# New durations in a list scheduler, a charge for changes of TensorE's tile configuration, and a mask matmul padded from 42 to 128 rows

## The chip, the core and the metric

The kernel runs on one core of one Trainium2 chip. The metric is device time in microseconds (us), the median of three executions of the whole kernel.

## What is computed

The reference is a two-layer backbone over 1024 latent tokens and 256 context tokens of width 1024, all in float32. Cut to one layer:

```python
u = modulate(rms_norm(h, norm1_g), mod[0], mod[1])          # latent and context, own modulation
pa, pb, pc, pd = split(u @ w_in)                            # four head groups
ya = ssd_bidir(conv_silu(pa))        # Mamba-2 SSD, chunks of 128, forward and backward
yb = block_attention(rope(rms_norm(q)), rope(rms_norm(k)), v)          # grouped-query, 4 heads
yc = gelu(gate) * (rglru(forward) + rglru(backward))        # RG-LRU, a linear scan
yd = diff_attention(q, k, v)         # softmax(q1 k1) v - lam * softmax(q2 k2) v, 4 heads
h = h + mod[2] * (concat(ya, yb, yc, yd) @ w_out)
h = h + mod[5] * (square(relu(modulate(rms_norm(h, norm2_g), mod[3], mod[4]) @ w_mlp1)) @ w_mlp2)
```

Inside the SSD each chunk needs `exp(a_cum[l] - a_cum[s])` under a triangular mask, and `exp(a_cum)` alone.

## The kernel before

Every float32 matrix is split into a high and a low part in a rounded format (`F32R`), and a product is the sum of three matmuls: high by high, high by low, low by high. `gemm_fm` and `gemm_tm` issue these in groups of three, 512 or 256 columns wide; the two layers hold 18,456 recorded matmuls. The other matmuls (transposes, SSD, P times V, sums of squares) stay in plain float32.

The program first records all operations in program order as a graph (`Sched.op`). Then `Sched.run` plays the graph through a model of five engines (PE is TensorE, DVE VectorE, ACT ScalarE, POOL GpSimd, SP the queue of DMA issues). At each model time every free engine takes, from the operations whose predecessors are done and whose buffers can be given, the one with the smallest latest start (`pri`, worked out backwards in `due` from TensorE's own order). The order in which operations are taken is the order in which the instructions are issued; on the chip each engine then works through its own list in that order, and semaphores enforce the dependencies. So the model's durations never become time directly. They only set the order on each engine, which engine takes an operation that either ACT or DVE can do (`either`), and which buffer a tile gets.

The model's prices stand in `act_cost`, `dve_cost`, `mm_cost` and `mms`; the latency from one engine to the next is the `gap` in `run` (0 on one engine, 200 ns where TensorE is on either side, else `LAT`), and `HOP` is the latency that `due` assumes. An operation that both ACT and DVE can do is skipped by one engine where the other would be done sooner, with ACT's duration weighted by 1.0 and DVE's by 1.6 (`PREF`).

A layer runs in this order, with neighbours overlapped as far as the graph and the buffers allow: norm, RG-LRU projections, RG-LRU, query, key and value projections, SSD for two groups, then attention in two rounds of one grouped-query and one differential head pair each (`G1D1`, `G0D0`), the output projection, norm, MLP. In time, layer 0's projections, LRU and SSD lie at about 20 to 450 us, its attention at 450 to 800, output projection and MLP (and the start of layer 1) up to about 1850; for layer 1 the same stretches are 1850 to 2250, 2250 to 2550, and 2550 to the end.

The mask matmul is in `ssd_group`, once per chunk of 128 tokens and group: `pick` (a column of an identity, in two copies, spread over 128 columns) times `acr`, which holds the cumulated decays, their high parts in rows 0 to 9 and their low parts in rows 32 to 41. It brings one chunk's row of decays to all 128 partitions. Its two operands are 42 rows high.

"Tile configuration" is the part of the 128 by 128 array that a matmul uses: its height is 32, 64 or 128 rows and its width 32, 64 or 128 columns, the next that holds the operand. Most matmuls are 128 by 128; P times V, parts of the SSD and of the attention's output use 64 columns, the sums of squares and the modulation 32 columns, the mask matmul 64 rows.

Of the kernel before, what the change touches and what calls it, by code (L numbers as in the profile page):

```python
# [11 lines left out]
F32R = mybir.dt.float32r  # L12
# [141 lines left out]


class Sched:
    LAT = 150.0
    HOP = 220.0
    STRETCH = 1.5
    TABLES = {AF.Sqrt: 1, AF.Exp: 0, AF.Tanh: 0, AF.Abs: 0}  # L160
    PREF = dict(ACT=1.0, DVE=1.6)
# [124 lines left out]
        self.ops.append(o)  # L286
        return o

# [1 line left out]
    def act_cost(self, out, in_, func, **kw):  # L290
        n = max(out.n(), in_.n())
        aps = sum(isinstance(kw.get(k), _V) for k in ("scale", "bias"))
        return (52 if in_.t.cls == "psum" else 94) + n / 1.2 + 93 * aps + (93 if "accum_out" in kw else 0)

    def act(self, out, in_, func, **kw):
        return self.op("ACT", [("activation", dict(out=out, in_=in_, func=func, **kw))],
# [2 lines left out]
    def dve_cost(self, method, fast=False, n=None, **kw):  # L299
        if n is None:  # L300
            n = max(x.n() for x in kw.values() if isinstance(x, _V))
        rate = 0.521 if fast else 1.0417
        if method == "reciprocal":
            rate = 6.25
        aps = sum(isinstance(kw.get(k), _V) for k in ("scalar", "scalar1", "scalar2"))
        return 69 + rate * n + 61 * aps

    def dve(self, method, fast=False, n=None, **kw):
        return self.op("DVE", [(method, kw)], self.dve_cost(method, fast, n, **kw))
# [56 lines left out]
    def mm_cost(self, rhs):  # L366
        n = rhs.n()
        if rhs.dt == F32R:
            return 2.5 + (n / 2.4 if n >= 256 else n * 4 / 2.4)
        return 2.5 + max(n * 4 / 2.4, 187)  # L370

    def mms(self, calls, par=1):
        cost = sum(self.mm_cost(c["rhs"]) for c in calls) / par
        return self.op("PE", [("matmul", c) for c in calls], cost + 10)

    def transposes(self, calls):
        return self.op("PE", [("transpose", c) for c in calls], 109.0 * len(calls))

# [1 line left out]
    def due(self):  # L380
        ops = self.ops
        end = [0.0] * len(ops)
# [31 lines left out]
    def run(self, trace=None):  # L414
        self.due()
        ops = self.ops
        n = len(ops)
# [26 lines left out]
        releases = []  # L444
        t = 0.0
        table = 0
        done = 0
        last_t = 0.0

# [37 lines left out]
        while done < n:  # L487
            progress = False
            while releases and releases[0][0] <= t:
                _, cn, slot, s = heapq.heappop(releases)  # L490
                c = self.classes[cn]
                c["live"][s] -= 1
                if cn == "psum":
                    c["busy"] = [None if x is slot else x for x in c["busy"]]
                else:
                    c["free"].append((t, slot))
            for e in names:
                if free[e] > t:
                    continue
                f = fut[e]  # L500
                while f and f[0][0] <= t:
                    _, pri, i = heapq.heappop(f)
                    if ops[i].t0 is None:
                        heapq.heappush(avail[e], (pri, i))
                skipped = []
                pick = None
                while avail[e]:
                    pri, i = heapq.heappop(avail[e])
                    if ops[i].t0 is not None:
                        continue  # L510
                    o = ops[i]
                    if any(max(t, free[a], o.ready[a]) + o.alts[a][1] * self.PREF[a] < t + o.alts[e][1] * self.PREF[e]
                           for a in o.alts if a != e):
                        skipped.append((pri, i))
                        continue
                    if not o.new or can_alloc(o):
                        pick = i
                        break
                    skipped.append((pri, i))
                for x in skipped:  # L520
                    heapq.heappush(avail[e], x)
                if pick is None:
                    continue
                o = ops[pick]
                o.eng = e
                o.calls, o.cost = o.alts[e]
                progress = True
                if e == "ACT":
                    need = self.TABLES.get(o.calls[0][1].get("func"))
                    if need is not None and need != table:  # L530
                        table = need
                        o.cost += 1283.0
                for tl in o.new:
                    self._alloc(tl)
                    if tl.cls != "dram":
                        c = self.classes[tl.cls]
                        c["live"][tl.stream] += 1
                        heads[tl.cls, tl.stream] += 1
                self._emit(o)
                o.t0 = t  # L540
                free[e] = t + o.cost
                if o.nbytes:
                    begin = max(dma_free, t + 1100)
                    dma_free = begin + o.nbytes / 360.0
                    end = dma_free + 850.0
                else:
                    end = t + o.cost
                if trace is not None:
                    trace.append((t, end, o))
                done += 1  # L550
                for j in start_succ[pick]:
                    p = ops[j]
                    p.left -= 1
                    for a in p.alts:
                        p.ready[a] = max(p.ready[a], t)
                        if p.left == 0:
                            heapq.heappush(fut[a], (p.ready[a], p.pri, j))
                for j in o.succs:
                    p = ops[j]
                    p.left -= 1  # L560
                    for a in p.alts:
                        gap = 0 if a == e and not o.nbytes else 200 if "PE" in (a, e) else self.LAT
                        p.ready[a] = max(p.ready[a], end + gap)
                        if p.left == 0:
                            heapq.heappush(fut[a], (p.ready[a], p.pri, j))
                for tl in o.tiles:
                    tl.ops_left -= 1
                    tl.end = max(tl.end, end)
                    if tl.ops_left == 0 and tl.slot is not None:
                        heapq.heappush(releases, (tl.end + self.LAT, tl.cls, tl if tl.cls == "psum" else tl.slot, tl.stream))  # L570
                last_t = max(last_t, end)
            if progress:
                continue
            nxt = [free[e] for e in names if free[e] > t and (avail[e] or fut[e])]
            nxt += [fut[e][0][0] for e in names if fut[e] and fut[e][0][0] > t]
            if releases:
                nxt.append(max(releases[0][0], t))
            nxt = [x for x in nxt if x > t]
            if not nxt:
                raise RuntimeError("no operation can be issued")  # L580
            t = min(nxt)
# [66 lines left out]
class Trunk:  # L648
# [23 lines left out]
        self.s.cls(cn, self.sb, 1, n)  # L672
        return self.s.tile(cn, n, dt, "", name, rows)

# [1 line left out]
    def setup(self):  # L676
        s, A = self.s, self.A
        self.cst = self.const(448, "cst")
        s.dma(self.cst.v, A["cst"])
        c = self.cst  # L680
        self.ident, self.mf, self.mb = c[:, 0:128], c[:, 128:256], c[:, 256:384]
        self.blk2, self.inv_ln, self.inv128 = c[:, 384:386], c[:, 386:387], c[:, 387:388]
        self.nhalf, self.tiny, self.ones32 = c[:, 388:404], c[:, 404:405], c[:, 406:438]
        self.pick = self.const(10, "pick", dt=F32R)[0:42, :]
        s.copy("DVE", self.pick, c[0:42, 438:448])
        self.cT = self.const(8 * 32, "cT")
        self.consts_a(0)
        x = s.tile("h", 512, F32, "load", "cx")
# [185 lines left out]
        b = 48 * si + 8 * m + k  # L874
        return self.L[l]["mod"][:, b:b + 1]

# [1 line left out]
    def split_w(self, raw, n):  # L878
        s = self.s
        hi = s.tile("w", WW, F32R, "", "wh")  # L880
# [55 lines left out]
                   dict(out=o, lhsT=ul, rhs=wh[:, b:b + m], start=False, stop=(k == 7))])  # L936
        return bank

# [1 line left out]
    def load_x(self, gi):  # L940
        s, A = self.s, self.A
        if gi == 0:
# [102 lines left out]
                s.dma(x[:, NL:NT], y[:, CO:CW].f)  # L1045
        self.mixd[k] = d

# [1 line left out]
    def conv(self, out, raw, wcols, bcol, W=CW):  # L1049
        s = self.s  # L1050
        o = out[:, 0:W]
# [24 lines left out]
             300)  # L1076
        return raw

# [1 line left out]
    def lru_weights(self, l):  # L1080
        s, A = self.s, self.A
        bd = s.tile("S", SW, F32, "lru", "bd")
# [69 lines left out]
        s.stt(wv, wv, 0.5, g, ALU.mult, ALU.mult)  # L1152
        self.split_mix(4 + ct, w, wy, "lru")

# [1 line left out]
    def ssd_dt(self, l, dtraw):  # L1156
        s, L = self.s, self.L[l]
        c = self.ssdc
# [16 lines left out]
        s.act(w1, w1, AF.Exp)  # L1175
        s.tt(te, w1, dt, ALU.mult)
        R = s.tile("S", SW, F32R, "ssdr", "acr")
        s.op("POOL", [("memset", dict(ap=R[0:42, 0:1024].f, constant=0.0))], 1300)
        n4 = nac.r("p (t d g h) -> p g d h t", t=10, d=2, g=2)
        for g in range(2):  # L1180
            pb = s.tile("psum", 512, F32, "ssd", "par")
# [8 lines left out]
    def ssd_group(self, l, g, xs, B, C, zmake):  # L1190
# [37 lines left out]
        for i, c in enumerate(order):  # L1228
# [3 lines left out]
            E, ex, cf = wk[:, 0:512], wk[:, 512:768], wk[:, 768:1024]  # L1232
            CE = E
            pb = s.tile("psum", 512, F32, "ssd", "pbc")
            s.mms([dict(out=pb.v, lhsT=self.pick[:, c:c + 1].bc([42, 128]), rhs=self.acr[0:42, 512 * g:512 * g + 512],
                        start=True, stop=True)])
            s.act(E, pb.v, AF.Exp)
            for hh in range(2):
# [54 lines left out]
            s.stt(yy, yy, L["sng"][:, g:g + 1], pb[:, 0:128 * n], ALU.mult, ALU.mult)  # L1293
        self.split_mix(g, y, W, "ssd")

# [1 line left out]
    def qk_post(self, l, bank, off, H, d, gain, t, dst, rq=None):  # L1297
        s = self.s
        n = H * d
# [71 lines left out]
        if name == "dtq":  # L1371
            self.ssd_dt(l, dtraw)

# [1 line left out]
    def att_open(self, l, kind, idx):  # L1375
        s, qd = self.s, self.qd
        gqa = kind == "gqa"
# [149 lines left out]
                yield (blk + i / len(sts)) / nblk  # L1527
                self.att_block(st, blk, nblk)

# [1 line left out]
    def out_proj(self, l, gis, ks):  # L1531
        s = self.s
        n = NT if l == 0 else NL
# [240 lines left out]
```

## Time and profile before

| | before |
|---|---|
| median of 3 executions | 3346.67 us (3345.6, 3346.67, 3353.66) |
| span of the profiled execution | 3352.2 us |
| time of the profiled execution | not listed apart; 3353.66 is the only one of the three that is longer than the span |
| TensorE busy | 3258.6 us (97%), 18,456 matmuls |
| VectorE busy | 2171.1 us (65%) |
| ScalarE busy | 1166.4 us (35%) |
| GpSimd busy | 147.1 us (4%) |
| mean granted clock of TensorE | 0.990 |

The profile is of one execution. A matmul's end is modelled: it is listed longer than the time until the next one starts, so neighbouring matmuls overlap in it, and a stretch in which TensorE counts as busy may still hold lost time. The distance from one start to the next shows what a matmul costs in a stream.

### The profile page before, as it was taken

To read this page: it belongs to the slowest core of one execution; us is meant where nothing else is said; L and a number is where in the kernel's file an instruction comes from. 1 tells how busy PE (TensorE), PEld (TensorE's weight loads), DVE (VectorE), ACT (ScalarE), POOL (GpSimd) and SP (SyncE) were. 2 spreads that over 40 slices of the span, in tenths; PEclk is the share of its full clock that TensorE was granted. 3 is DMA by queue.
4 is the path that set the end of the run, shared out by engine and by line. 5 is a ranking of instruction groups with operands and counts; after the bars stand their busy time and mean duration, and the time that the engine had idled before them with its cause. 6 is when DMAs were issued, how large, how long until landed. Compare 5 with 4: busy or idle time off the path is not lost. (4 is left out here: it accounts for less than half of the span.)

```text
span 3352.2 us, 45841 instructions
## 1 busy us (share of the span) xinstructions
PE 3258.6 (97%) x18456; PEld 2622.8 (78%) x18456; DVE 2171.1 (65%) x3785; ACT 1166.4 (35%) x2026; POOL 147.1 (4%) x168
## 2 busy tenths in 40 slices
PE   8999989999999999999999999999999999999999
PEld 6877786677688888887887888886677788888887
DVE  4787789894565555554556688689883655555554
ACT  5554447772311110101112554438771311111111
POOL 0010040000000000000000010030000000000000
PEclk9999999999999999999999989989999999999999
DMA  8443261416212222212110321151433111111111
GB/s 247 140 125 97 89 175 41 110 35 232 70 48 75 72 79 67 78 57 85 42 45 26 118 73 50 57 154 39 97 116 121 41 51 51 51 44 46 49 50 57
DMA packets 253868, 276.51 MB, mean 82 GB/s; under 512 B 22876, under 2 KB 212184, under 8 KB 253656
## 3 DMA queue, kind: packets, MB, share of 16 engines
q1 hardware_dynamic: 253656, 273.59, 27.0%
q8 instruction: 145, 2.38, 0.3%
q14 instruction: 67, 0.55, 0.1%
HBM read 218.75 MB, written 54.79 MB: 82 GB/s over the span
## 5 line engine op out<-in xcount | busy, mean ns | idle before, releaser
L606 DVE SCALAR_TENSOR_TENSOR hR<-banks,mod,hR 128x512 f32<-128x512 f32 x720 | 497.2, 697 | 420.4 <-PE banks L606 420.4
L606 PE MATMUL banks<-uh,wh 128*128 128x512 f32 (+1 forms) x1808 | 682.4, 377 | 5.8 <-ACT cvr L606 1.9
L606 PE MATMUL banks<-uh,wl 128*128 128x512 f32 (+1 forms) x1808 | 669.1, 370 | 1.7 <-DVE wl L606 1.7
L606 PE MATMUL banks<-ul,wh 128*128 128x512 f32 (+1 forms) x1808 | 669.0, 370 | 1.3 <-DVE ul L606 1.2
L606 ACT ACTIVATE wh<-wr 128x1024 fp32r<-128x1024 f32 (+2 forms) x193 | 189.5, 992 | 1050.7 <-PE banks L606 1009.9
L606 PE MATMUL banks<-hh,wh 128*128 128x512 f32 (+1 forms) x1280 | 476.7, 372 | 0.0
L606 PE MATMUL banks<-hl,wh 128*128 128x512 f32 (+1 forms) x1280 | 475.5, 371 | 0.0
L606 PE MATMUL banks<-hh,wl 128*128 128x512 f32 (+1 forms) x1280 | 474.8, 371 | 0.0
L606 PEld LDWEIGHTS banks<-uh,wh 128*128 128x128 f32 x1808 | 341.3, 189 | 98.8 <-issue 26.1
L606 PEld LDWEIGHTS banks<-uh,wl 128*128 128x128 f32 x1808 | 340.6, 188 | 65.4 <-DVE wl L606 3.0
L606 PEld LDWEIGHTS banks<-ul,wh 128*128 128x128 f32 x1808 | 341.1, 189 | 61.5 <-DVE ul L606 3.7
L606 DVE TENSOR_SCALAR_CACHE_REDUCE P<-banks,rq 128x1280 f32<-128x1280 f32 (+1 forms) x216 | 301.3, 1427 | 29.4 <-PE banks L606 28.1
L606 DVE TENSOR_TENSOR r<-r 128x512 f32<-128x512 f32 x160 | 102.2, 639 | 333.6 <-ACT r L606 331.4
L606 PEld LDWEIGHTS banks<-hh,wh 128*128 128x128 f32 x1280 | 240.8, 188 | 53.5 <-DVE hR L606 5.3
L606 ACT ACTIVATE P<-P,am 128x1280 f32<-128x1280 f32 (+1 forms) x216 | 273.4, 1272 | 21.1 <-DVE P L606 19.8
L606 PEld LDWEIGHTS banks<-hh,wl 128*128 128x128 f32 x1280 | 240.4, 188 | 44.7
L606 PEld LDWEIGHTS banks<-hl,wh 128*128 128x128 f32 x1280 | 240.6, 188 | 43.3
L606 PE MATMUL banks<-wh,uh 128*128 128x256 f32 (+2 forms) x784 | 250.4, 319 | 6.0 <-DVE qkw L606 4.2
L606 DVE TENSOR_TENSOR wl<-wr,wh 128x1024 fp32r<-128x1024 f32 (+2 forms) x204 | 230.4, 1137 | 27.6 <-ACT wh L606 26.1
L606 PE MATMUL banks<-ks,qt 128*128 128x512 f32 (+1 forms) x800 | 220.8, 387 | 20.2 <-DVE P L606 15.7
L606 PE MATMUL banks<-wl,uh 128*128 128x256 f32 (+2 forms) x784 | 226.3, 289 | 0.0
L606 PE MATMUL banks<-wh,ul 128*128 128x256 f32 (+2 forms) x784 | 225.5, 288 | 0.0
(241 smaller groups left out, 4341.0 us busy)
## 6 DMA issues: line engine op xcount, KB each, us to landing
wr<-in_w_mlp_dram SPq DMA_DIRECT2D x128, 512.0 KB
wm<-in_w_mod_dram SPq DMA_DIRECT2D x96, 512.0 KB
wr<-in_w_in_dram SPq DMA_DIRECT2D x40, 512.0 KB
ks<-dk SPq DMA_DIRECT2D x64, 160.0 KB
qt<-dq SPq DMA_DIRECT2D x72, 128.0 KB
wr<-in_w_out_dram SPq DMA_DIRECT2D x64, 128.0 KB
hd<-hT SPq DMA_DIRECT2D x8, 640.0 KB
ks<-gk SPq DMA_DIRECT2D x16, 320.0 KB
```

What stands on the lines that cost most here:

```text
L606: getattr(e, method)(**args)
```

## The change

Three things change. The scheduler's prices and latencies are replaced (`LAT`, `HOP`, the constants in the cost functions, the gap from TensorE 200 ns and to TensorE 55 ns, the time after which a freed buffer can be given again). A matmul group whose tile configuration differs from the one before it on TensorE is charged `SWITCH` = 190 ns more; this is added after the group has been chosen. And `pick` and `acr` become 128 rows high, with zeros in the rows that were not used, so that the mask matmul runs in the 128 by 128 configuration. The cut diff (comment lines removed by the change are left out):

```diff
-    LAT = 150.0
-    HOP = 220.0
+    LAT = 35.0
+    HOP = 150.0
+    DRAIN = 200.0
+    SWITCH = 190.0
...
-        return (52 if in_.t.cls == "psum" else 94) + n / 1.2 + 93 * aps + (93 if "accum_out" in kw else 0)
+        return (169 if in_.t.cls == "psum" else 205) + n / 1.2 + 90 * aps + (200 if "accum_out" in kw else 0)
...
+        elif method == "tensor_tensor_scan":
+            rate = 2.13
...
-        return 69 + rate * n + 61 * aps
+        return 157 + rate * n + 57 * aps + (83 if "accum_out" in kw else 0)
...
         if rhs.dt == F32R:
-            return 2.5 + (n / 2.4 if n >= 256 else n * 4 / 2.4)
-        return 2.5 + max(n * 4 / 2.4, 187)
+            return max(4 + n * 0.4453, 112)
+        return max(5 + n * 4 / 2.4, 216)
...
-        return self.op("PE", [("matmul", c) for c in calls], cost + 10)
+        return self.op("PE", [("matmul", c) for c in calls], cost)
...
+    @staticmethod
+    def mode(o):
+        method, c = o.calls[0]
+        x = c["lhsT"] if method == "matmul" else c["in_"]
+        up = lambda n: 32 if n <= 32 else 64 if n <= 64 else 128
+        return up(x.shape[0]), up(x.shape[1])
...
+                if e == "PE":
+                    m = self.mode(o)
+                    if m != mode:
+                        mode = m
+                        o.cost += self.SWITCH
...
-                        gap = 0 if a == e and not o.nbytes else 200 if "PE" in (a, e) else self.LAT
+                        gap = 0 if a == e and not o.nbytes else self.DRAIN if e == "PE" else 55 if a == "PE" else self.LAT
...
-                        heapq.heappush(releases, (tl.end + self.LAT, tl.cls, tl if tl.cls == "psum" else tl.slot, tl.stream))
+                        heapq.heappush(releases, (tl.end + (self.DRAIN if e == "PE" else 55), tl.cls, tl if tl.cls == "psum" else tl.slot, tl.stream))
...
-        self.pick = self.const(10, "pick", dt=F32R)[0:42, :]
-        s.copy("DVE", self.pick, c[0:42, 438:448])
+        self.pick = self.const(10, "pick", dt=F32R)
+        s.copy("DVE", self.pick.v, c[:, 438:448])
...
-        s.op("POOL", [("memset", dict(ap=R[0:42, 0:1024].f, constant=0.0))], 1300)
+        s.op("POOL", [("memset", dict(ap=R[:, 0:1024].f, constant=0.0))], 1300)
...
-            s.mms([dict(out=pb.v, lhsT=self.pick[:, c:c + 1].bc([42, 128]), rhs=self.acr[0:42, 512 * g:512 * g + 512],
+            s.mms([dict(out=pb.v, lhsT=self.pick[:, c:c + 1].bc([128, 128]), rhs=self.acr[:, 512 * g:512 * g + 512],
```

## Rows read from the trace of the kernel before

**Rows 1.** The page: span, and busy time by engine.
```profile
span 3352.2 us, 45841 instructions
PE 3258.6 (97%) x18456; PEld 2622.8 (78%) x18456; DVE 2171.1 (65%) x3785; ACT 1166.4 (35%) x2026; POOL 147.1 (4%) x168
```

**Rows 2.** Busy time by stretch: length, engines, granted clock, DMA share, GB/s.
```profile
20.00:450.00 430.00, 412.55 (x2751) 338.09 (x2750) 324.29 (x693) 215.17 (x427) 43.94 (x67) 0.98 0.43 132
450.00:800.00 350.00, 326.81 (x2374) 252.37 (x2374) 298.55 (x558) 236.24 (x432) 31.79 (x19) 1.00 0.38 114
800.00:1850.00 1050.00, 1047.85 (x5435) 848.25 (x5434) 563.21 (x915) 166.37 (x242) 5.41 (x12) 1.00 0.21 66
1850.00:2250.00 400.00, 383.61 (x2398) 329.77 (x2397) 308.19 (x653) 188.43 (x375) 52.24 (x57) 0.95 0.30 89
2250.00:2550.00 300.00, 281.75 (x1955) 210.25 (x1954) 249.17 (x385) 209.78 (x348) 10.19 (x6) 0.99 0.33 99
2650.00:3352.00 702.00, 697.45 (x3035) 564.32 (x3033) 373.00 (x499) 108.23 (x137) 0.00 (x0) 1.00 0.17 49
```

**Rows 3.** The same view of thirteen stretches at the lower clock.
```profile
154.50:158.00 3.50, 3.50 (x10) 2.03 (x10) 0.40 (x1) 0.69 (x1) 0.00 (x0) 0.52 1.00 344
...
2253.70:2257.20 3.50, 3.50 (x14) 3.00 (x13) 3.33 (x6) 1.06 (x2) 2.01 (x1) 0.52 0.68 192
sum 65.90, PE 61.55 PEld 53.27 DVE 48.03 ACT 29.40 POOL 16.95; mean PE 4.73 PEld 4.10 DVE 3.69 ACT 2.26 POOL 1.30
```

**Rows 4.** Waits of TensorE by releaser: us in total, times, longest.
```profile
PE banks L606 <- DVE P L606: 18.1, 38, 1.5
PE banks L606 <- ACT PT L606: 12.3, 37, 0.9
PE banks L606 <- DVE qkw L606: 10.0, 9, 2.5
PE banks L606 <- DVE wk L606: 7.1, 6, 3.8
```

**Rows 5.** Timeline of TensorE around one mask matmul.
```profile
300.59 0.39 PE L606 MATMUL banks<-uh,wh 128*128 128x512 f32 x1
300.82 0.40 PE L606 MATMUL banks<-ul,wh 128*128 128x512 f32 x1
301.06 0.39 PE L606 MATMUL banks<-uh,wl 128*128 128x512 f32 x1
301.38 0.50 PE L606 MATMUL banks<-acr,pick 42*128 42x512 f32 x1
301.81 0.51 PE L606 MATMUL banks<-uh,wh 128*128 128x512 f32 x1
302.15 0.39 PE L606 MATMUL banks<-ul,wh 128*128 128x512 f32 x1
302.38 0.39 PE L606 MATMUL banks<-uh,wl 128*128 128x512 f32 x1
```

**Rows 6.** The instructions on `pick`: duration min/median/max, first and last start.
```profile
L606 PE MATMUL banks<-acr,pick x36: 489/497/742, 263.4 to 2193.2; 42*128 42x512 f32 x36
L606 DVE CAST pick<-cst x1: 165/165/165, 3.4 to 3.4; 42x10 fp32r<-42x10 f32 x1
```

**Rows 7.** Groups of GpSimd instructions: count, busy us, mean ns, idle before.
```profile
L606 POOL MEMSET bd<- 128x1024 f32 x2 | 1.9, 952 | 1.0 <-PE banks L606 1.0
L606 POOL MEMSET acr<- 42x1024 f32 x2 | 1.9, 948 | 0.0
```

**Rows 8.** Timeline of ScalarE, then of VectorE, in layer 1's attention.
```profile
2262.93 1.36 ACT L606 ACTIVATE P<-P,am 128x1280 f32<-128x1280 f32 x1
2264.18 0.20 ACT L606 ACTIVATION_READ_ACCUMULATOR P<-P,am 128x1 f32 x1
2264.28 1.36 ACT L606 ACTIVATE P<-P,am 128x1280 f32<-128x1280 f32 x1
...
2263.70 1.55 DVE L606 TENSOR_SCALAR_CACHE_REDUCE P<-banks,rq 128x1280 f32<-128x1280 f32 x1 [0.43 <-PE banks L606]
2265.18 0.08 DVE L606 DVE_READ_ACCUMULATOR P<-banks,rq 128x1 f32 x1
2265.18 1.55 DVE L606 TENSOR_SCALAR_CACHE_REDUCE P<-banks,rq 128x1280 f32<-128x1280 f32 x1
```

**Rows 9.** Instructions on `PT`, the copies of transposed P: duration min/median/max, forms.
```profile
L606 ACT ACTIVATE PT<-banks x259: 575/597/639, 493.4 to 2520.5; 128x512 f32<-128x512 f32 x130
L606 DVE COPY PT<-banks x69: 679/687/694, 512.7 to 2508.6; 128x512 f32<-128x512 f32 x69
```

**Rows 10.** Timeline of VectorE and TensorE where a projection's transposes wait.
```profile
2197.64 1.22 DVE L606 SCALAR_TENSOR_TENSOR z<-B,z 128x1024 f32<-128x1024 f32 x1
...
2199.15 1.23 DVE L606 TENSOR_TENSOR xs<-xs,z 128x1024 f32<-128x1024 f32 x1
2200.29 0.42 DVE L606 TENSOR_TENSOR qkw<-qkw,qkm 128x256 f32<-128x256 f32 x1
...
2200.77 0.48 PE L606 MATMUL banks<-cst,qkw 128*128 128x128 f32 x1 [2.52 <-DVE qkw L606]
```

More of the change, by code (lines that the diff above doesn't have):

```diff
@@ L446, in run @@
         table = 0
+        mode = None
         done = 0
```

## The prediction

> **What bounds the kernel now.** I read the page first: TensorE is busy 97% of the span, VectorE 65%, ScalarE 35% [rows 1]. So time goes where TensorE loses it, and the busy time by stretch says where [rows 2]. The two MLP stretches, 800 to 1850 and 2650 to 3352 us, have 2.2 and 4.6 us without TensorE: 1752 us that no order can shorten by much. What is left lies in four stretches. Projections, LRU and SSD (20 to 450 and 1850 to 2250) leave TensorE idle for 17.5 and 16.4 us; the attentions (450 to 800 and 2250 to 2550) for 23.2 and 18.3 us, with VectorE busy for 85% and 83% of them. That is 75 us. There is a second loss: thirteen stretches at the lower granted clock, 1.2 instead of 2.4 GHz, together 65.9 us, in which TensorE was busy for 61.6 us [rows 3]. At the higher level the same work takes about half, so some 30 us are lost there. Nearly all of it lies in the projection and SSD stretches, whose granted clock is 0.98 and 0.95 against 1.00 in the MLP [rows 2]; it fell after waits such as the one of 3.8 us for `wk` and that of 2.5 us for `qkw` [rows 4]. The waits by releaser show what TensorE waits for: results of VectorE in short chains, `P`, `qkw`, `wk`, and ScalarE's copies `PT` [rows 4].
>
> **The padding.** The mask matmul is 512 columns wide in the rounded format, like its neighbours. Among full-size matmuls one starts every 0.23 to 0.24 us (300.59, 300.82, 301.06); around the mask matmul the distances are 0.32, 0.43 and 0.34 [rows 5]. That is 1.09 us for three, where three ordinary ones take 0.70: 0.39 us more, for two changes of configuration, about 0.195 us each (which is what `SWITCH` charges). There are 36 mask matmuls, from 263.4 to 2193.2 us [rows 6]. In the timeline 26 of them stand between two full-size matmuls and lose both changes; nine have a narrow matmul (64 or 32 columns) on one side, so one change stays there anyway, and one has narrow ones on both sides and keeps two. That removes 26 x 2 + 9 = 61 changes, 61 x 0.195 = 12 us. The bounds are 0, if TensorE only waits longer for the same VectorE results, and 36 x 0.39 = 14 us. I take 12, since TensorE is busy for 96% of these stretches. What the padding adds is nothing that shows: the copy of `pick` is one instruction of 0.17 us near the start [rows 6]; GpSimd's memset of `acr` takes 948 ns for 42 rows, and a memset of 128 rows and the same width takes 952 [rows 7]. The matmul streams the same 512 columns.
>
> A rule of the Trainium skill speaks against this term: "TensorE: Matmul & The Clock Gate", section "Why this matters for your kernels", says that a single matmul of 32 contraction rows takes the same time as one of 128. By that rule the padding gains nothing and the sum below would be 3335. The rows, 0.43 us beside 0.23, do not agree for a low matmul between full ones.
>
> **The charge for changes.** `SWITCH` is added after a group has been picked, so the list does not prefer groups of the same configuration. It only makes the model's TensorE arrive later. I give it no term of its own: apart from the 61, the number of changes stays.
>
> **The prices.** Three comparisons of price and trace decide what the new order can be worth.
>
> TensorE: a 512-column matmul was priced at 216 ns (plus 3 for its third of the group's 10); now 232. The trace has 230 to 240 [rows 5]. The new price is right, the old one 7% short.
>
> ScalarE and VectorE, in attention: one softmax pass of 1280 columns was priced at 94 + 1067 + 93 + 93 = 1347 ns on ScalarE, now 205 + 1067 + 90 + 200 = 1562. The instructions last 1.36 and 0.20 us, but one pass starts 1.35 us after the one before (2262.93 to 2264.28): an instruction begins before its predecessor has ended [rows 8]. On VectorE the old price is 69 + 1333 + 61 = 1463, the new 157 + 1333 + 57 + 83 = 1630; the distance in the trace is 1.48 us (2263.70 to 2265.18) [rows 8]. So as occupancy the old prices were right to 1%, and the new ones are 16% and 10% too long. The new ones are right for latency, and the shorter gaps (35 and 55 ns instead of 150 and 200) give most of it back: a VectorE result of 512 columns reaches TensorE after 69 + 533 + 200 = 802 ns before and 157 + 533 + 55 = 745 after.
>
> Thus the change makes TensorE right, chains inside one engine longer (as they are), and streams of independent operations too slow. In the projection and SSD stretches the waits come from chains behind long operations: VectorE works on `z` and `xs`, 1.2 us each, while the transposes of `qkw` wait 2.5 us [rows 10]. Later model results let the list put other matmuls ahead of those that must wait. What can be won there is 17.5 + 16.4 idle and some 30 of low clock, 64 us together. No row shows what a new order does with it. The bounds I set are six tenths of it (-40: the clock stretches go with the waits that precede them) and a fifth more of it (+12: another order with waits of the same kind). I take a fifth, -12, nearer to the weak end, because the old prices were already close.
>
> In attention there is little for an order to find: VectorE is the busiest engine there but for TensorE itself, so a better order of TensorE's work waits for the same results. The bounds are -12 (a quarter to a third of the 41 us idle) and +22 (32 more `PT` copies on VectorE at 0.69 us, see below). I take 0.
>
> **The sum.** -12 (padding) -12 (waits and clock) +0 (attention) +0 (MLP) = -24 us. The profiled execution has a span of 3352.2 us; if it is the run of 3353.66, 1.5 us lie around it, and the sum gives 3329.7 for its like. The median is 7 us below that run, and from the median of 3346.7 I get 3323. A measurement of this kernel cannot tell a difference under about 0.3% (10 us) from none.
>
> **Rivals.**
> *The waits go, and the clock with them.* For it: the low stretches stand behind single waits, so one wait removed gives back more than its length. Against it: there are many short chains, and an order that mends one can hurt the next. Padding -12, waits and clock -40, attention -8: 3287.
>
> *Nothing that can be told.* The order is another, not a better one, and the 12 us of the padding are given back as waits in the same SSD chain (TensorE waits for `wk` there [rows 4]): -12 + 9 = 3344. This is also the case in which the change does not do what it says, since only orders change. For it: the old prices were right to 1% where VectorE is fullest [rows 8].
>
> *Slower: copies go to VectorE.* The place is attention, and the mechanism is the choice between ScalarE and VectorE for the `PT` copies. VectorE now does 69 of 328 [rows 9]. In the model a block of one grouped-query and one differential pair costs ScalarE 6 x 1347 + 10 x 479 = 12.9 us before and 6 x 1562 + 10 x 596 = 15.3 after; VectorE, 8 passes of 1463 = 11.7 before and 6 x 1630 + 2 x 1547 = 12.9 after. The model's ScalarE fills up by 2.5 us, VectorE by 1.2, so more copies are offered to VectorE, which on the chip is the fuller one [rows 2]. Each costs it up to 0.69 us [rows 9]. If the waits elsewhere give nothing, 18 more copies eat the padding's 12 us and 32 make the kernel slower by 10; 50 more give -12 + 35 = +23, 3370. Against it: VectorE also pauses in these stretches and could hide some.
>
> What makes this rival possible is a rule of the Trainium skill, "ScalarE: Activation LUTs", section "What ACT_TABLE_LOAD costs": back-to-back ACTIVATEs overlap by about 93 ns. By that rule a duration is not an occupancy; the trace agrees, with 0.10 to 0.11 us (1.36 long, the next one 1.25 later [rows 8]).
>
> **How the numbers follow.** The forecast case (3300 to 3336, point 3323) has a chance of 0.45, the first rival 0.19, no change 0.19, slower 0.17. So faster 0.64, same 0.19, slower 0.17. The range takes in the first rival's point and the bounds of the forecast (-12 and -12 with a further -43, and the slower case up to its threshold of +10): 3280 to 3358, leaving out about 0.08 below and 0.12 above.
>
> **What would show it.** Padding: the mask matmul as 128 rows, distances around it at 0.23 to 0.24 where its neighbours are full-size. Waits: less than 34 us of TensorE idle in the two projection and SSD stretches, and less than 66 us at the lower clock. Attention: idle still near 41 us, and the count of `PT` copies on VectorE near 69; well over 100 would mean the slower rival. MLP: the same 1752 us. Wrong would be the forecast if the idle time moved by more than 30 us either way, or if the lower clock appeared in the MLP.

## The result, and the profile after

The changed kernel takes 3445.84 us (median of 4) against 3350.16 us for the kernel before in the same comparison: 1.028 times as long, 95% interval 1.0258 to 1.0302. It is slower by 2.8%, where 0.7% faster was forecast.

The page of the changed kernel, span and busy time by engine (before: [rows 1]):

```profile
span 3443.2 us, 45870 instructions
PE 3290.3 (96%) x18456; PEld 2649.2 (77%) x18456; DVE 2140.7 (62%) x3695; ACT 1217.9 (35%) x2116; POOL 152.2 (4%) x168
```

The work is the same, 18,456 matmuls; 90 instructions have moved from VectorE to ScalarE. The profiled executions differ by 91.0 us (3443.2 against 3352.2). To see where they went, the timelines of both kernels give the starts of the first score matmul and of the last matmul of P and V in each layer: 485.0, 782.1, 2249.5 and 2526.0 us before; 513.7, 835.3, 2320.5 and 2617.1 after. So the projections, LRU and SSD of layer 0 lose 28.7 us, its attention 24.5, the stretch up to layer 1's attention 17.8, that attention 20.1, and the rest nothing. The busy time by stretch, with bounds moved along with the work (columns as in [rows 2], which has the same six stretches before):

```profile
20.00:478.00 458.00, 428.21 (x2795) 351.14 (x2795) 332.35 (x709) 216.59 (x426) 44.23 (x69) 0.95 0.41 125
478.00:853.00 375.00, 335.08 (x2333) 259.49 (x2332) 291.87 (x542) 241.82 (x433) 29.22 (x18) 0.95 0.35 104
853.00:1907.00 1054.00, 1051.06 (x5446) 851.09 (x5444) 546.22 (x861) 190.48 (x296) 5.97 (x12) 1.00 0.21 66
1907.00:2321.00 414.00, 382.52 (x2393) 330.26 (x2392) 308.00 (x650) 190.47 (x377) 59.46 (x56) 0.94 0.28 84
2321.00:2641.00 320.00, 288.48 (x1952) 213.88 (x1952) 245.01 (x378) 215.63 (x352) 9.82 (x6) 0.97 0.32 96
2741.00:3443.00 702.00, 697.51 (x3036) 564.43 (x3034) 362.16 (x469) 120.85 (x169) 0.00 (x0) 1.00 0.17 50
```

TensorE's idle time, length minus its busy time, is now 29.8 and 31.5 us in the two projection stretches and 39.9 and 31.5 in the attentions: 133 us instead of 75. The MLPs are as they were. The granted clock has fallen in the attentions too, to 0.95 and 0.97. The 25 stretches at the lower level (1.2 GHz) inside the work, the first and the sum:

```profile
31.70:38.60 6.90, 6.72 (x15) 3.95 (x15) 4.72 (x9) 3.38 (x7) 0.00 (x0) 0.51 1.04 323
...
sum 146.70, PE 128.75 PEld 101.91 DVE 96.66 ACT 54.61 POOL 30.13; mean PE 5.15 PEld 4.08 DVE 3.87 ACT 2.18 POOL 1.21
```

TensorE was busy for 129 us at half speed, against 61.6 in [rows 3]: by estimate (half of the busy time) about 64 us lost instead of 31. So 57 us more of idle time and some 33 more of lower clock, together the 91. Who TensorE waits for (us in total, times, longest; before: [rows 4]):

```profile
PE banks L623 <- ACT PT L623: 29.7, 50, 1.2
PE banks L623 <- DVE P L623: 19.6, 44, 1.3
PE banks L623 <- DVE wk L623: 13.8, 17, 2.6
PE banks L623 <- DVE qkw L623: 11.8, 7, 4.2
PE banks L623 <- DMA qt<-gq: 9.4, 2, 5.3
```

Each old wait has grown in total, that for `P` by little, and a new one has come: queries that are written out and read back (`qt` from `gq`) land too late for the first scores of layer 1's attention (5.3 us) and once in layer 0's (4.2 us).

The mask matmul does what it should. TensorE's timeline around one:

```profile
422.97 0.28 PE L623 MATMUL banks<-wh,ul 128*128 128x256 f32 x1
423.09 0.40 PE L623 MATMUL banks<-acr,pick 128*128 128x512 f32 x1
423.32 0.28 PE L623 MATMUL banks<-wh,uh 128*128 128x256 f32 x1
423.44 0.28 PE L623 MATMUL banks<-wl,uh 128*128 128x256 f32 x1
```

It now takes 0.23 us from its start to the next, and its neighbour, half as wide, 0.12: no change of configuration is left around it (0.32, 0.43 and 0.34 in [rows 5]).

In the attention VectorE waits as well. Its waits for the scores of a softmax pass, in the kernel before and then in the changed one (us in total, times, longest):

```profile
DVE P L606 <- PE banks L606: 28.1, 28, 3.8
```

```profile
DVE P L623 <- PE banks L623: 84.9, 39, 10.6
```

The longest of them in the timeline of the changed kernel, VectorE's rows and then TensorE's:

```profile
2506.63 0.15 DVE L623 RECIPROCAL fac<-am 128x2 f32<-128x2 f32 x1
2517.36 1.55 DVE L623 TENSOR_SCALAR_CACHE_REDUCE P<-banks,rq 128x1280 f32<-128x1280 f32 x1 [10.58 <-PE banks L623]
...
2504.98 4.33 PE L623 MATMUL banks<-PT,V 128*64 128x256 f32 x32
2509.24 0.66 PE L623 MATMUL banks<-cst,P 128*128 128x128 f32 x4
2509.65 0.48 PE L623 MATMUL banks<-ks,qt 128*128 128x512 f32 x1
2510.06 4.54 PE L623 MATMUL banks<-PT,V 128*64 128x256 f32 x40
...
2516.96 0.49 PE L623 MATMUL banks<-ks,qt 128*128 128x256 f32 x2
```

TensorE did not pause here. It worked on P times V and transposes and had the scores (`ks,qt`), for which VectorE stood idle for 10.6 us, behind them in its list. What such a pause costs TensorE is not seen here; the fifth round below shows that the time of a kernel does not follow these waits.

### The profile page after: what moved, and what is told of

The parts are those of the page before. It is cut to its first block, busy times and chain, and to the rows that moved or that the text cites. A ratio compares the mean times of both kernels' runs of the same rounds, so it can differ in the third digit from the quotient of the medians.

```text
span 3443.2 us, 45870 instructions
## 1 busy us (share of the span) xinstructions
PE 3290.3 (96%) x18456; PEld 2649.2 (77%) x18456; DVE 2140.7 (62%) x3695; ACT 1217.9 (35%) x2116; POOL 152.2 (4%) x168
## 5 line engine op out<-in xcount | busy, mean ns | idle before, releaser
L623 ACT ACTIVATE wh<-wr 128x1024 fp32r<-128x1024 f32 (+2 forms) x156 | 150.0, 975 | 952.1 <-PE banks L623 767.2
L623 ACT ACTIVATE P<-P,am 128x1280 f32<-128x1280 f32 (+1 forms) x216 | 272.7, 1265 | 30.5 <-DVE P L623 28.7
L623 PE MATMUL banks<-ks,qt 128*128 128x512 f32 (+1 forms) x800 | 228.2, 401 | 31.5 <-DVE P L623 17.5
L623 PE MATMUL banks<-cst,P 128*128 128x128 f32 x1312 | 201.4, 285 | 40.2 <-ACT PT L623 27.5
```

Of the source, the lines that this page charges most:

```text
L623: getattr(e, method)(**args)
```

## The experiments

The time of each kernel is compared with runs of the kernel before on the same chip; ratios have 95% intervals. "Over the padding" means the difference of the ratio to that of `pad_only`, times 3350 us. The theories at first: A, the new prices of VectorE and ScalarE mislead the list; B, TensorE's new price and charge do; C, the order of before was singled out, and any other costs about as much.

**The parts of the change, first round.** `pad_only` has the four padding lines of the diff and nothing else. `pad_pe` adds `mm_cost`, `mms` and the charge (`SWITCH`). `pad_engines` has the padding and the other half: `act_cost`, `dve_cost`, `LAT`, the gaps, the releases, `HOP`. `jitter_before` is the kernel before with

```diff
 def op(self, eng, calls, cost, nbytes=0):
+    cost *= 1 + 0.02 * ((7919 * len(self.ops) + 0) % 101 / 100 - 0.5)
```

For an operation that either engine can do, the factor reaches its priority only; its prices in the model's clock stay.

`pad_only`: 

> The kernel before with the padded mask matmul alone; prices and order are those of before. Both theories (the loss comes from the engines' prices; the loss comes from any new order) expect that the padding itself is not the cause: 61 changes of configuration fewer at 0.195 us, 12 us faster, 3330 to 3340 us. If the loss came from the padding, it would be near 3440.

3341.77 us, ratio 0.9969 (0.9957 to 0.9981): 10.5 us faster. It is the fastest kernel of the study.

`pad_pe`: 

> Padding, TensorE's new prices and the charge for changes; VectorE, ScalarE, latencies and HOP as before. Theory A (VectorE's and ScalarE's durations taken as occupancy, with shortened latencies, mislead the list): no loss here, 3320 to 3350 us. Theory B (a slower TensorE in the model moves the order the wrong way): near 3440. Theory C (the old order was singled out, any other costs about as much): 3400 to 3440 too.

3391.98 us, 1.0125 (1.0110 to 1.0140): 52 us over the padding, between what theory A and theories B and C expected.

`pad_engines`: 

> Padding, the new prices of VectorE and ScalarE, the new gaps and HOP; TensorE's prices as before, no charge for changes. Theory A: most of the loss is here, 3410 to 3450 us. Theory B: 3320 to 3350. Theory C: 3400 to 3440.

3441.14 us, 1.0271 (1.0256 to 1.0286): 101 us over the padding, nearly all that the changed kernel loses. Theory A's number, but the half of B costs too. The two halves do not add: the changed kernel, which has both, is 104 us over the padding.

`jitter_before`: 

> The kernel before, without padding, each operation's price multiplied by a fixed number between 0.99 and 1.01 that depends on its place in the program: no price is better or worse, but the order is another. Theory C: 1 to 3% slower, 3380 to 3440 us. Theories A and B: within 0.5% of before, 3335 to 3365.

3359.23 us, 1.0025 (1.0013 to 1.0036): 8 us slower. Theory C in this form falls: an order that differs at random by small errors costs little.

**Each part alone, second round**, all on top of the padding: `pad_price` has the diff's `act_cost` and `dve_cost`, `pad_lat` its `LAT`, gaps and releases, `pad_mm` its `mm_cost` and `mms`, `pad_switch` its charge.

`pad_price`: 

> Padding and the new prices of VectorE and ScalarE alone (gaps, HOP, TensorE as before). Theory A1 (durations taken as occupancy mislead the list): most of the 99 us that the engines' part costs over the padding alone is here, 3400 to 3450 us. Theory A2 (the shortened gaps and earlier release of buffers take away slack): close to the padding alone, 3335 to 3365.

3414.21 us, 1.0181 (1.0166 to 1.0196): 71 us over the padding.

`pad_lat`: 

> Padding and the shorter gaps and releases alone (35 and 55 ns instead of 150 and 200), prices and HOP as before. Theory A2: 3400 to 3450 us. Theory A1: 3335 to 3365, since the gaps alone move little.

3371.00 us, 1.0052 (1.0037 to 1.0067): 28 us.

`pad_mm`: 

> Padding and TensorE's new matmul prices alone (512 columns 232 ns instead of 216 plus 3), no charge for changes. If the 50 us of TensorE's part come from a model TensorE that is slower and so needs its results later, they are here: 3375 to 3400 us. If they come from the charge, 3335 to 3360.

3381.10 us, 1.0076 (1.0060 to 1.0093): 36 us.

`pad_switch`: 

> Padding and the charge of 190 ns for each change alone, TensorE's prices as before. If the charge is the cause of TensorE's 50 us: 3375 to 3400 us. If the prices are: 3335 to 3360.

3377.54 us, 1.0071 (1.0056 to 1.0086): 34 us. No single part carries the loss. All four cost, the engines' prices twice as much as any other, and again they do not add: 169 us one by one, 104 together.

**What the engines' prices do, third round.** They act in two places: in the priorities (`due`) and in the model's clock (`run`). With `extra` the difference of the new price to the old, on top of the padding:

```diff
 # price_pri, in due
-    c = o.cost * self.STRETCH
+    c = (o.cost + self.extra(o.eng, o.calls)) * self.STRETCH
...
 # price_clock, in run, after self.due()
+    for o in ops:
+        o.alts = {a: (c, x + self.extra(a, c)) for a, (c, x) in o.alts.items()}
...
 # price_down, in act_cost and dve_cost
-        return (52 if in_.t.cls == "psum" else 94) + n / 1.2 + 93 * aps + (93 if "accum_out" in kw else 0)
+        return (8 if in_.t.cls == "psum" else 50) + n / 1.2 + 93 * aps + (93 if "accum_out" in kw else 0)
...
-        return 69 + rate * n + 61 * aps
+        return 25 + rate * n + 61 * aps
```

`jitter10` is `pad_only` with the line of `jitter_before` and 0.2 in place of 0.02.

`price_clock`: 

> The padded kernel, new VectorE and ScalarE prices in the model's clock alone; the priorities are worked out with the old prices. The new prices cost 72 us over the padding alone when they are in both. If the harm is in the clock (the list believes the two engines busier than they are and takes other work first): 3395 to 3425 us. If it is in the priorities: 3335 to 3360.

3411.66 us, 1.0169 (1.0152 to 1.0186): 67 us over the padding, nearly the whole of the 71 of `pad_price`.

`price_pri`: 

> The reverse: new VectorE and ScalarE prices in the priorities alone, old ones in the model's clock. Harm in the priorities: 3395 to 3425 us. Harm in the clock: 3335 to 3360.

3376.63 us, 1.0065 (1.0046 to 1.0084): 32 us, neither of the two numbers.

`price_down`: 

> The padded kernel with VectorE's and ScalarE's prices 44 ns lower than before, so wrong the other way by about half as much. Direction theory (a model that believes the engines too slow makes the worse order): equal to the padding alone or faster, 3320 to 3350 us. Tuned-point theory (the old prices were the best of their kind, any consistent shift costs): 3360 to 3390.

3383.61 us, 1.0085 (1.0070 to 1.0100): 39 us. Prices that are wrong the other way cost as well, so it is not a matter of the sign alone.

`jitter10`: 

> The padded kernel, each price multiplied by a fixed number between 0.9 and 1.1 by its place in the program: errors about as large as the change's for a short operation, but of both signs. If any large shift of prices costs as much as the change's: 3380 to 3420 us. If only a shift of one sign does: 3340 to 3365.

3381.83 us, 1.0076 (1.0060 to 1.0093): 36 us. By their sizes there are two losses: some 30 to 40 us that quite different shifts of the prices cost alike, and as much again where the engines' higher prices are in the clock.

**Duration or occupancy, fourth round.** In the model an engine is free again after the full price. In the trace the next instruction starts before the last one's end [rows 8]. `after_split` is the changed kernel with the two kept apart; `price_split` is `pad_price` with the same lines:

```diff
+    def lap(a, calls):
+        acc = "accum_out" in calls[0][1]
+        return {"ACT": 110 * (1 + acc), "DVE": 84 + 66 * acc}.get(a, 0)
...
-                free[e] = t + o.cost
+                free[e] = t + o.cost - self.lap(e, o.calls)
```

`jitter10b` is `jitter10` with 50 in place of 0 in its line, which moves each factor up or down by half of its range.

`after_split`: 

> The changed kernel in all its prices, but in the model an engine is free again after the measured distance of starts (84 ns less than the price on VectorE, 110 on ScalarE, 150 and 220 for a pass with a sum), while results still take the full price. If occupancy is the cause of the further loss: 3375 to 3410 us. If it is not: 3430 to 3450, as the changed kernel.

3353.63 us, 1.0004 (0.9994 to 1.0013): 92 us less than the changed kernel, faster than either range expected. Everything else of the change is still in it.

`price_split`: 

> The padded kernel with the new VectorE and ScalarE prices (3414 us in pad_price), freed early in the same way. Occupancy the cause: 3365 to 3390 us, like the other shifts. Not the cause: 3400 to 3420.

3378.14 us, 1.0072 (1.0055 to 1.0088): back at what the other shifts cost.

`jitter10b`: 

> A second draw of jitter10 (3382 us): the same errors of up to a tenth on each price, dealt to other operations. If any order of that kind costs 30 to 40 us over the padding alone: 3365 to 3395 us. If jitter10 was an accident: 3335 to 3355.

3365.28 us, 1.0041 (1.0027 to 1.0055): 24 us over the padding, less than the first draw's 36. Errors of a tenth cost, by the draw, three to four and a half times what errors of a hundredth did.

**Which engine, fifth round.** `split_dve` and `split_act` are `after_split` with only one of the two entries in `lap`; `split_hop` has `HOP = 220.0` again.

`split_dve`: 

> after_split with VectorE alone freed early, ScalarE's full duration counted as occupancy. If VectorE's occupancy is what matters, being the busiest engine after TensorE: 3350 to 3375 us. If ScalarE's: 3415 to 3445.

3360.40 us, 1.0023 (1.0012 to 1.0033).

`split_act`: 

> after_split with ScalarE alone freed early, VectorE's full duration counted as occupancy. If VectorE's occupancy is what matters: 3405 to 3445 us. If ScalarE's: 3350 to 3375. If both share: both of these runs near 3400.

3445.27 us, 1.0279 (1.0264 to 1.0295): ScalarE's occupancy put right gives nothing back; VectorE's gives nearly all. VectorE's waits for scores do not explain it. In `split_dve`, then in `after_split`, then in `split_act` (columns as above):

```profile
DVE P L628 <- PE banks L628: 33.1, 23, 2.9
```

```profile
DVE P L628 <- PE banks L628: 59.9, 38, 6.5
```

```profile
DVE P L628 <- PE banks L628: 76.0, 51, 6.2
```

`after_split` waits twice as long as the kernel before (28.1 us) and takes the same time, and `price_clock`, with 29.2 us of such waits, is 67 us over the padding. What does go with the time is TensorE's wait for `wk`, which VectorE finishes in the SSD, chunk by chunk; in the same order:

```profile
PE banks L628 <- DVE wk L628: 3.6, 5, 1.1
```

```profile
PE banks L628 <- DVE wk L628: 2.3, 3, 0.9
```

```profile
PE banks L628 <- DVE wk L628: 17.7, 21, 2.3
```

In the five kernels whose model holds VectorE for the whole of its raised price (the changed one, `pad_engines`, `pad_price`, `price_clock`, `split_act`) these waits are 13.8 to 17.7 us in all, in the others, the kernel before among them, at most 9.0. The same five are 67 to 104 us over the padding, all others that have it at most 52. The place agrees: the starts that were 513.7, 835.3, 2320.5 and 2617.1 us in the changed kernel are 483.5, 798.5, 2246.9 and 2529.7 in `split_dve`. The way to the two attentions gives back 30.2 and 36.8 us, the attentions 6.6 and 13.8; the rest is 3.5 longer.

The sum over the stretches at the lower clock, in `after_split` and then in `split_act`:

```profile
sum 51.10, PE 46.10 PEld 37.91 DVE 33.18 ACT 15.22 POOL 13.55; mean PE 4.61 PEld 3.79 DVE 3.32 ACT 1.52 POOL 1.36
```

```profile
sum 129.60, PE 109.25 PEld 88.47 DVE 89.05 ACT 54.91 POOL 19.27; mean PE 4.75 PEld 3.85 DVE 3.87 ACT 2.39 POOL 0.84
```

With both occupancies right, the lower clock is at the level of the kernel before (65.9 us in [rows 3]); with ScalarE's alone it stays near the changed kernel's.

`split_hop`: 

> after_split with HOP at 220 again. If HOP is what is left: 3335 to 3345 us. If not: within 0.5% of after_split, 3340 to 3370.

3373.84 us, 1.0067 (1.0049 to 1.0086): 21 us slower than `after_split` (1.0067 against 1.0004), outside both ranges. The shorter `HOP` is not what is left of the loss; going back to the longer one costs again.

## Why the prediction was wrong

**What bounds the kernel** was read rightly: the MLPs kept their time, and the whole loss lies in the stretches named, as idle time and lower clock.

**The padding** was right: -12 us forecast, -10.5 measured alone (interval -6 to -14). The trace of `pad_only` has 368 changes of configuration, that of the kernel before 429: the 61 fewer that were counted. The Trainium skill ("TensorE: Matmul & The Clock Gate", section "Why this matters for your kernels") states that a single matmul of 32 rows takes the same time as one of 128. By that rule the padding would have given 0, which lies outside that interval; how a low matmul does among low ones no run here shows.

**The charge and TensorE's price** were given no term, because the charge steers no choice directly and the price is the true one. Alone, each costs 34 to 36 us over the padding, so "It only makes the model's TensorE arrive later" was wrongly taken as nothing: what the list takes next depends on when results are ready in the model. But this is not what made the changed kernel slow. Without this half the loss over the padding is 101 us (`pad_engines`), with it 104, and `after_split`, which has it too, is 12 us over the padding.

**The engines' prices** hold the step that failed. The prediction saw that the old prices were VectorE's and ScalarE's occupancy to 1% and the new ones 10 and 16% too long. It then took that as a small error on the safe side: "Later model results let the list put other matmuls ahead of those that must wait", worth -12 in the projections (bounds -40 and +12) and 0 in the attention (-12 and +22). Before and after, the way to the two attentions differs by 28.7 + 17.8 = +46.5 us with the padding's gain in it, so about +57 without it where -12 was taken, and the attentions themselves by 24.5 + 20.1 = +44.6. Both lie far over the bounds. The prediction's own sign of being wrong came: idle time moved by more than 30 us, by 57.

That VectorE's price as occupancy is the cause is shown: of the 96 us that the changed kernel is slower, `after_split` takes back 92 and `split_dve` 86, `split_act` nothing. How the wrong occupancy turns into lost time is seen in part: most of what comes back lies before the attentions, and there TensorE's waits for `wk` go with it. But these waits are only 10 us of it (13.8 against 3.6 in `split_dve`). Where the list puts things wrongly in the attentions, and how the rest of the loss comes about, stays open.

**The slower rival** had the right sign and the right rule behind it and the wrong place. The Trainium skill ("ScalarE: Activation LUTs", section "What ACT_TABLE_LOAD costs") states that back-to-back ACTIVATEs overlap; VectorE's instructions do so here, 1.55 us long and 1.48 apart [rows 8]. So a duration is not an occupancy. But the rival put the harm into copies that ScalarE hands to VectorE. They went the other way, as the instructions on `PT` in the changed kernel show (before: [rows 9]):

```profile
L623 ACT ACTIVATE PT<-banks x268: 574/597/607, 522.4 to 2611.7; 128x512 f32<-128x512 f32 x134
L623 DVE COPY PT<-banks x60: 671/687/695, 541.0 to 2597.4; 128x512 f32<-128x512 f32 x60
```

60 on VectorE instead of 69. Nor does the time follow this count: it is 99 in `split_dve`, 46 in `after_split`, 30 in `split_act`. And ScalarE's overprice, on which that rival rested too, does little harm where VectorE's occupancy is right (`split_dve` keeps it and is at 1.0023).

**What stays open.** Quite different shifts of the prices (`pad_lat`, `pad_mm`, `pad_switch`, `price_pri`, `price_down`, two draws of a tenth) each cost 24 to 39 us over the padding, and errors of a hundredth 8 us against the kernel before. Why the old constants give a better order than each of these is not settled; that they had been fitted on this program would explain it and was not tried. Nor is it settled why `after_split`, with prices nearer to the trace than before's, is no better than before, and 12 us behind the padding alone. With orders that differ by 24 to 39 us for such shifts, some of what `after_split` and `split_dve` give back may be luck of the order; that `price_split` gives back 36 us in the same way speaks for the cause. Of the diff the padding alone is worth keeping: 0.9969.

## What to carry to other kernels

A list scheduler needs two numbers for an instruction: how long the engine is taken (the distance of starts in a stream) and how long the result takes (the duration). Putting the second in place of the first on the busiest helper engine, by some 84 ns per instruction, accounts for 86 of the 96 us that this order lost, though the new prices agree with the durations in the trace (a `PT` copy on VectorE, priced at 157 + 533 = 690 ns, lasts 687 [rows 9]). And a model that is more accurate in one price is not a better order: change one price at a time and time the kernel, because the greedy list answered every shift tried here with another time.

## What the runs showed of the hardware

The lower clock added more than half as much as the waits did. One stretch of the kernel before, with its attention of layer 0, and one of the changed kernel, where layer 1's attention begins (columns as in [rows 2]):

```profile
493.00:1967.00 1474.00, 1447.93 (x8164) 1155.82 (x8162) 908.62 (x1478) 455.36 (x736) 18.22 (x21) 1.00 0.24 75
```

```profile
2320.00:2331.00 11.00, 9.02 (x31) 7.11 (x31) 6.51 (x11) 3.73 (x6) 1.64 (x1) 0.59 0.63 172
```

Before, the granted clock did not fall for 1474 us, though TensorE waited 59 times in them, the longest for 1.7 us. After, it fell within the wait of 5.3 us for `qt` and is at 0.59 in the 11 us that begin with its end: 7.1 us of TensorE's work lie at half speed there. In all, TensorE's time at 1.2 GHz rose from 61.6 to 128.8 us. Such a wait costs more than its length, and a new order that makes some pays twice. Not every stretch at the lower level begins at a long wait: the one at 711.0 us of the changed kernel comes behind four of 0.55 to 0.69 us.
